# Moving the transposes' transfers off ScalarE's queue in a one-core encoder layer

## The chip, the cores and the metric

The kernel runs on one core of a Trainium2 chip. The metric is the device time of one execution in microseconds. Three runs of the kernel before took 1799.64, 1800.62 and 1801.30 us; the median is 1800.62 us.

## The reference

One encoder layer over 256 tokens of width 2048, all in float32:

```python
x = x + 0.5 * swiglu(rms_norm(x, ffn1_norm), ffn1_w_gu, ffn1_w_down)     # D_FF = 5632
proj = rms_norm(x, mix_norm) @ w_in                                      # 2048 x 4608
out_a = grouped-query attention, 8 query and 2 key heads of 128, q and k normed and rotated
out_b = differential attention, 4 heads: softmax map 0 minus lam * softmax map 1, o normed
x = x + concat(out_a, out_b) @ w_out
x = x + 0.5 * swiglu(rms_norm(x, ffn2_norm), ffn2_w_gu, ffn2_w_down)
x = rms_norm(x, out_norm)
```

Attention is bidirectional without a mask. All weights are read once, about 338 MB.

## The kernel before

**Matrix products.** Every float32 operand is split into a rounded part `hi` and a rest `lo`, and each product is three matmuls (lines 192 to 194): hi by hi, hi by lo, lo by hi. `mm_block` works on a block of the weights, 1024 columns wide. It goes through it in chunks of 256 rows: SyncE's queue (SP) loads a chunk (`raw`, line 173, three buffers), ScalarE (ACT) casts its two halves to `whi` (line 126, four buffers), VectorE (DVE) subtracts to get `wlo` (line 127), and TensorE (PE) runs 24 matmuls of 512 columns over it: two column halves, two token tiles, two row halves, three products.

**Interleaving.** Work that is not a matmul of the weights stands in a list, `pending`. `mm_block` takes entries from its front while it goes on: `slots` a chunk, 1 in the feed-forward parts and `MIX_SLOTS` in the mixer (`pump`). An empty entry (`lambda: None`) only spaces the list. The order of each engine's instructions is then set by a planner that simulates the engines and their queues, so an entry's place in the list is a priority rather than a fixed place. `issue_after(ins)` holds an instruction behind `ins` on its own engine. Each engine and each queue runs its instructions in the order that was written, and waits at the first one that is not ready.

**Transposes.** The activations `h` of the feed-forward part and the heads `q` and `k` of the mixer have to be turned. DVE transposes blocks of 32 by 32 (`turn`, lines 271 and 449), DMAs move the blocks between partitions (`move`, lines 277 and 453), and a copy or a split puts them in order (`order`, line 457; `parts`). ACT's queue begins all of these DMAs: 16 for each of the 12 groups of `h`, and 16 for each of the six head tiles (two token tiles of q of group A, k of group B and q of group B). The buffer `near` of the heads is single, so the second tile's transpose waits until the first tile's DMAs have read it.

**The mixer.** Its projection blocks run in the order k and v of A, q of A, k of B, q of B, v of B. After the last chunk of a block `qk_heads` norms and rotates the heads (ACT, DVE and GpSimd (POOL) in turn), and their turn is put into `pending`, to be done while the next block's matmuls run. The attention's stages (`scores`, `probs`, `values`, and `turn` for B) follow in the same list.

Of the kernel before, what the change touches and what calls it, by code (L numbers as in the profile page):

```python
# [28 lines left out]
B32 = 32  # L29
Q = P // B32  # L30
# [5 lines left out]
LAMBDA_INIT = 0.8 - 0.6 * math.exp(-0.3 * 0)  # L36
WB = 1024
WARM = 8
MIX_SLOTS = 3


@with_exitstack
def encoder_layer(ctx: ExitStack, tc: tile.TileContext, a: dict, out: bass.AP):
# [3 lines left out]
    nc = tc.nc  # L47
# [11 lines left out]
    def f32(ap):  # L59
        return ap.bitcast(F32)  # L60
# [22 lines left out]

    pending = collections.deque()

    def pump():
        if pending:
            pending.popleft()()

    def drain():  # L90
        while pending:
            pump()
# [30 lines left out]
                nc.gpsimd.tensor_tensor(self.rstd[t], ms, minus_half[:, :1], op=ALU.pow)  # L123

    def split(hi, lo, src):
        nc.scalar.copy(hi, src)  # L126
        return nc.vector.tensor_tensor(lo, src, f32(hi), op=ALU.subtract)  # L127

    def new_xT():
# [15 lines left out]
                nc.vector.scalar_tensor_tensor(lo[:, k + j, :], pj, gk, f32(hi[:, k + j, :]),  # L145
                                               op0=ALU.mult, op1=ALU.subtract)

    loads, splits = [], []

    def late_load(dst, src):  # L150

# [74 lines left out]
    def add_to_x(half, scale):  # L226
        def evac(b, t, ps, c0=0, c1=512):
            s = slice(half * WB + b * 512 + c0, half * WB + b * 512 + c1)
            nc.vector.scalar_tensor_tensor(x[t][:, s], ps[:, c0:c1], scale, x[t][:, s],  # L229
                                           op0=ALU.mult, op1=ALU.add)  # L230
        return evac


    def ffn(xT, norm, w_gu, w_down, half_done=None, before=None, after=None, last_evac=None, t_major=None):
        with tc.tile_pool(name="ffn", bufs=2) as fp:
            groups = [(c, min(WB, DFF - c)) for c in range(0, DFF, WB)]

            def gate(j):
                c, width = groups[j]
                sg = [fp.tile([P, WB], F32, name=f"sg{t}", bufs=1) for t in range(NT)]  # L240

                def evac(b, t, ps):
                    nc.scalar.activation(sg[t][:, b * 512:(b + 1) * 512], ps, AF.Silu,  # L243
                                         scale=norm.rstd[t][:, 0:1])
                if j == 0 and before is not None:
                    with tc.manual_schedule(engines={mybir.EngineType.SP}):
                        mm_block(xT, NK, w_gu, 0, c, width, evac, before, after)
                else:
                    mm_block(xT, NK, w_gu, 0, c, width, evac)
                return sg  # L250

            def up(j, sg):
                c, width = groups[j]
                h = [fp.tile([P, WB], F32, name=f"h{t}") for t in range(NT)]

                def evac(b, t, ps):
                    s = slice(b * 512, (b + 1) * 512)
                    nc.vector.scalar_tensor_tensor(h[t][:, s], ps, norm.rstd[t][:, 0:1], sg[t][:, s],  # L258
                                                   op0=ALU.mult, op1=ALU.mult)
                mm_block(xT, NK, w_gu, 0, DFF + c, width, evac)  # L260
                hT = (ht_p.tile([P, WB // P, T], F32R, name="hT_hi"),
                      ht_p.tile([P, WB // P, T], F32R, name="hT_lo"))
                nk = width // P
                n_ = nk * B32
                near = fp.tile([P, NT, Q, WB // Q], F32, name="near", bufs=1)[:, :, :, :n_]
                turned = fp.tile([P, NT, Q, WB // Q], F32, name="turned", bufs=1)[:, :, :, :n_]

                def turn(t):

                    with tc.issue_after(splits[-1].ins):  # L270
                        nc.vector.transpose(near[:, t].rearrange("p q (k d) -> p q k d", d=B32),  # L271
                                            h[t][:, :width].rearrange("p (k q d) -> p q k d", q=Q, d=B32))

                def move(i0):

                    for i, q in itertools.product(range(i0, i0 + 2), range(Q)):
                        nc.scalar.dma_start(turned[q * B32:(q + 1) * B32, :, i, :],
                                            near[i * B32:(i + 1) * B32, :, q, :])

                def parts(k):  # L280
                    src = turned.rearrange("p t i (k d) -> p (t i) k d", d=B32)[:, :, k:k + 2, :]
                    hi, lo = (part[:, k:k + 2, :].rearrange("p k (i d) -> p i k d", d=B32) for part in hT)
                    with tc.issue_after(splits[-1].ins):
                        split(hi, lo, src)

                pending.extend(functools.partial(turn, t) for t in range(NT))
                pending.append(lambda: None)
                pending.extend(functools.partial(move, i) for i in (0, 2))
                pending.append(lambda: None)
                pending.extend(functools.partial(parts, k) for k in range(0, nk, 2))  # L290
                pending.append(lambda: turned_groups.add(j))
                return hT

            def down(j, hT):
                c, width = groups[j]
                last = j == len(groups) - 1
                while j not in turned_groups:
                    pump()
                for half in range(2):
                    evac = last_evac(half) if last and last_evac else add_to_x(half, 0.5)  # L300
                    mm_block(hT, width // P, w_down, c, half * WB, WB, evac,
                             t_major=t_major if last and half == 1 else None)
                    if last and half_done:
                        half_done(half)

            n = len(groups)
            hT = {}
            turned_groups = set()
            for j in range(n):
                sg = gate(j)  # L310
                hT[j] = up(j, sg)
                if 0 < j < n - 1:
                    down(j - 1, hT.pop(j - 1))
            down(n - 2, hT.pop(n - 2))
            down(n - 1, hT.pop(n - 1))
# [39 lines left out]
    with ExitStack() as mixer:  # L355
# [86 lines left out]
        def turn_heads(o, dst):  # L442

            near = mw.tile([P, Q, 8, B32], F32, name="near", bufs=1)
            far = o.rearrange("p h d -> p (h d)").rearrange("p (i n) -> p i n", i=Q)

            def turn():
                with tc.issue_after(splits[-1].ins):
                    nc.vector.transpose(near, o.rearrange("p h (q d) -> p q h d", d=B32))

            def move():
                for i, q in itertools.product(range(Q), range(Q)):
                    nc.scalar.dma_start(far[q * B32:(q + 1) * B32, i],  # L453
                                      near[i * B32:(i + 1) * B32, q].rearrange("p h d -> p (h d)"))

            def order():
                nc.scalar.copy(dst.rearrange("p h (i d) -> p h i d", d=B32),
                               far.rearrange("p i (h d) -> p h i d", d=B32))
            pending.extend([turn, lambda: None, move, lambda: None, order])

        ka = []

# [141 lines left out]
        def new_oT():  # L604
            return (ht_p.tile([P, WB // P, T], F32R, name="hT_hi"),
                    ht_p.tile([P, WB // P, T], F32R, name="hT_lo"))

        w_in = a["w_in"]
        mm_block(xT2, NK, w_in, 0, 1024, 512, evac_kva, slots=MIX_SLOTS)
        mm_block(xT2, NK, w_in, 0, 0, WB, evac_qk("a", "q", qTa), slots=MIX_SLOTS)  # L610
        oTa = new_oT()
        s_, p_, v_ = zip(*[attn_a(h2, oTa) for h2 in range(4)])
        pending.extend([s_[0], s_[1], p_[0], s_[2], p_[1], v_[0], s_[3], p_[2], v_[1], p_[3], v_[2], v_[3]])
        mm_block(xT2, NK, w_in, 0, 2560, WB, evac_qk("b", "k", kTb), slots=MIX_SLOTS)
        qTb = mp.tile([P, 8, T], F32, name="qT")
        mm_block(xT2, NK, w_in, 0, 1536, WB, evac_qk("b", "q", qTb), slots=MIX_SLOTS)
        oTb = new_oT()
        s_, p_, v_, o_ = zip(*[attn_b(h, qTb, oTb) for h in range(4)])
        pending.extend([s_[0], s_[1], p_[0], s_[2], p_[1], s_[3], p_[2], p_[3]])
        mm_block(xT2, NK, w_in, 0, 3584, WB, evac_vb, slots=MIX_SLOTS)  # L620
        pending.extend([v_[0], v_[1], o_[0], v_[2], o_[1], v_[3], o_[2], o_[3]])
        for half in range(2):
            mm_block(oTa, 8, a["w_out"], 0, half * WB, WB, add_to_x(half, 1.0), slots=MIX_SLOTS)
        drain()
# [92 lines left out]
```

## Time and profile before

| | |
|---|---|
| median of three runs | 1800.62 us |
| the profiled execution | 1800.14 us |
| its span, first to last instruction | 1798.3 us |
| PE busy | 1775.8 us, 99% |
| DVE busy | 991.2 us, 55% |
| ACT busy | 829.2 us, 46% |
| POOL busy | 48.2 us, 3% |
| mean granted TensorE clock | 0.994 |

A busy share says how long an engine had an instruction at work. Matmuls are pipelined, so their durations overlap; their rate is read from how many start in a stretch. The granted clock is a share of full speed: 1.00 is 2.4 GHz. DMA-issuing instructions are not counted as busy time; in a timeline they stand under the engine's queue (ACTq, SPq). The mixer lies between about 735 and 1060 us of the span.

### The profile page before, as it was taken

To read this page: it belongs to the slowest core of one execution; us is meant where nothing else is said; L and a number is where in the kernel's file an instruction comes from. 1 tells how busy PE (TensorE), PEld (TensorE's weight loads), DVE (VectorE), ACT (ScalarE), POOL (GpSimd) and SP (SyncE) were. 2 spreads that over 40 slices of the span, in tenths; PEclk is the share of its full clock that TensorE was granted. 3 is DMA by queue.
4 is the path that set the end of the run, shared out by engine and by line. 5 is a ranking of instruction groups with operands and counts; after the bars stand their busy time and mean duration, and the time that the engine had idled before them with its cause. 6 is when DMAs were issued, how large, how long until landed. Compare 5 with 4: busy or idle time off the path is not lost.

```text
span 1798.3 us, 20478 instructions
## 1 busy us (share of the span) xinstructions
PE 1775.8 (99%) x7864; PEld 1466.0 (82%) x7864; DVE 991.2 (55%) x1147; ACT 829.2 (46%) x1195; POOL 48.2 (3%) x75
## 2 busy tenths in 40 slices
PE   9999999999999999999989999999999999999998
PEld 7888888888888888887778888888888888888886
DVE  6454645645545657754455664545645645545556
ACT  6443443443443444655766454343443443444444
POOL 0000000000000000130120000000000000000000
PEclk9999999999999999998999999999999999999999
DMA  9565655655656575655444455666656656656573
GB/s 343 195 210 190 223 196 188 213 198 196 212 193 206 164 242 188 211 168 184 162 156 173 165 186 187 197 216 205 202 191 210 207 188 214 204 190 211 153 253 121
DMA packets 117635, 355.73 MB, mean 198 GB/s; under 512 B 10992, under 2 KB 27808, under 8 KB 117408
## 3 DMA queue, kind: packets, MB, share of 16 engines
q1 hardware_dynamic: 96752, 338.39, 56.6%
q10 hardware_dynamic: 20688, 16.01, 3.2%
q8 instruction: 61, 1.00, 0.2%
q14 instruction: 38, 0.31, 0.1%
q0 software_dynamic: 96, 0.02, 0.0%
HBM read 337.60 MB, written 2.10 MB: 189 GB/s over the span
## 4 chain that ended last, share of the span: by engine, by line
PE 94%; ACT 2%; DMA 1%; DVE 1%; issue 1%; ACTq 0%; POOL 0%; DVEq 0%; POOLq 0%
PE psm L193 31%; PE psm L194 31%; PE psm L192 31%; DMA raw<-in_w_in 1%; ACT heads L422 0%; DVE wlo L127 0%; ACT whi L126 0%; DMA raw<-in_w_out 0%; PE psx L139 0%; PE psx L580 0%; ACT heads L440 0%; ACTq L453 0%; PE psx L525 0%; PE psx L560 0%; PE psx L545 0%
## 5 line engine op out<-in xcount | busy, mean ns | idle before, releaser
L127 DVE TENSOR_TENSOR wlo<-raw,whi 128x1024 fp32r<-128x1024 f32 (+1 forms) x676 | 756.7, 1153 | 683.7 <-ACT whi L126 680.0
L126 ACT CAST whi<-raw 128x1024 fp32r<-128x1024 f32 (+1 forms) x676 | 646.9, 996 | 818.8 <-PE psm L194 725.1
L193 PE MATMUL psm<-wlo,xT_hi 128*128 128x512 f32 x1696 | 662.4, 392 | 2.6 <-DVE wlo L127 2.5
L194 PE MATMUL psm<-whi,xT_lo 128*128 128x512 f32 x1696 | 659.0, 391 | 0.0
L192 PE MATMUL psm<-whi,xT_hi 128*128 128x512 f32 x1696 | 586.6, 392 | 9.1 <-ACT whi L126 7.7
L192 PEld LDWEIGHTS psm<-whi,xT_hi 128*128 128x128 f32 x1696 | 319.5, 189 | 77.8 <-ACT whi L126 9.2
L193 PEld LDWEIGHTS psm<-wlo,xT_hi 128*128 128x128 f32 x1696 | 319.7, 189 | 71.5 <-DVE wlo L127 5.2
L194 PEld LDWEIGHTS psm<-whi,xT_lo 128*128 128x128 f32 x1696 | 319.6, 188 | 66.0
L193 PE MATMUL psm<-wlo,hT_hi 128*128 128x512 f32 x836 | 323.4, 389 | 0.0
L194 PE MATMUL psm<-whi,hT_lo 128*128 128x512 f32 x836 | 323.4, 389 | 0.0
L192 PE MATMUL psm<-whi,hT_hi 128*128 128x512 f32 x836 | 293.8, 388 | 0.0
L193 PEld LDWEIGHTS psm<-wlo,hT_hi 128*128 128x128 f32 x836 | 157.0, 188 | 32.3
L192 PEld LDWEIGHTS psm<-whi,hT_hi 128*128 128x128 f32 x836 | 157.0, 188 | 32.1
L194 PEld LDWEIGHTS psm<-whi,hT_lo 128*128 128x128 f32 x836 | 157.0, 188 | 31.9
L229 DVE SCALAR_TENSOR_TENSOR x<-psm,x 128x512 f32<-128x512 f32 (+1 forms) x113 | 73.9, 680 | 16.0 <-PE psm L194 15.0
L123 POOL TENSOR_TENSOR rstd<-ms,minus_half 128x1 f32<-128x1 f32 x8 | 4.6, 575 | 1487.1 <-DVE ms L122 1487.1
L126 ACT CAST hT_hi<-turned 128x512 fp32r<-128x512 f32 x44 | 24.1, 617 | 39.2 <-DMA turned<-near 39.2
L243 ACT ACTIVATE sg<-psm,rstd 128x512 f32<-128x512 f32 x44 | 28.6, 687 | 12.5 <-PE psm L194 12.5
L258 DVE SCALAR_TENSOR_TENSOR h<-psm,rstd,sg 128x512 f32<-128x512 f32 x44 | 31.6, 737 | 0.0
L127 DVE TENSOR_TENSOR hT_lo<-turned,hT_hi 128x512 fp32r<-128x512 f32 x44 | 30.1, 684 | 0.0
L501 ACT ACTIVATE e<-psx,nb 128x256 f32<-128x256 f32 x32 | 14.8, 472 | 29.4 <-DMA heads<-near 24.7
L271 DVE STREAM_TRANSPOSE near<-h 128x1024 f32<-128x1024 f32 (+1 forms) x24 | 27.6, 1151 | 0.3
(101 smaller groups left out, 386.4 us busy)
## 6 DMA issues: line engine op xcount, KB each, us to landing
raw<-in_ffn_w_gu SPq DMA_DIRECT2D x158, 1024.0 KB, 5.0
raw<-in_ffn_w_down SPq DMA_DIRECT2D x88, 1024.0 KB, 5.0
raw<-in_w_in SPq DMA_DIRECT2D x32, 1024.0 KB, 5.2
raw<-in_ffn_w_gu SPq DMA_DIRECT2D x32, 512.0 KB, 3.7
raw<-in_w_out SPq DMA_DIRECT2D x16, 1024.0 KB, 4.9
turned<-near ACTq DMA_DIRECT2D x160, 64.0 KB, 4.2
raw<-in_w_in SPq DMA_DIRECT2D x8, 512.0 KB, 3.7
heads<-near ACTq DMA_DIRECT2D x96, 32.0 KB, 3.1
```

Source lines behind the costliest of these rows:

```text
L123: nc.gpsimd.tensor_tensor(self.rstd[t], ms, minus_half[:, :1], op=ALU.pow)
L126: nc.scalar.copy(hi, src)
L127: return nc.vector.tensor_tensor(lo, src, f32(hi), op=ALU.subtract)
L192: nc.tensor.matmul(o, xh, wh, start=k == 0, stop=False)
L193: nc.tensor.matmul(o, xh, wl, start=False, stop=False)
L194: nc.tensor.matmul(o, xl, wh, start=False, stop=k == nk - 1)
L229: nc.vector.scalar_tensor_tensor(x[t][:, s], ps[:, c0:c1], scale, x[t][:, s], op0=ALU.mult, op1=ALU.add)
L243: nc.scalar.activation(sg[t][:, b * 512:(b + 1) * 512], ps, AF.Silu, scale=norm.rstd[t][:, 0:1])
L258: nc.vector.scalar_tensor_tensor(h[t][:, s], ps, norm.rstd[t][:, 0:1], sg[t][:, s], op0=ALU.mult, op1=ALU.mult)
L271: nc.vector.transpose(near[:, t].rearrange("p q (k d) -> p q k d", d=B32), h[t][:, :width].rearrange("p (k q d) -> p q k d", q=Q, d=B32))
L501: nc.scalar.activation(e[:, m, :], sv[:, m, :], AF.Exp, bias=nb[:, m:m + 1], scale=SCALE, accum_out=sm[:, m:m + 1])
```

## The change

`h`'s DMAs are begun by POOL's queue, and the heads' DMAs by SP's, which carries the weight loads too. The heads' 16 DMAs become four entries of four instead of one entry, with three empty entries behind them, and the final copy is held behind ACT's latest cast. `MIX_SLOTS` goes from 3 to 4, and the attention's lists get empty entries. The number and the size of the transfers, and all arithmetic, stay as they are.

```diff
-MIX_SLOTS = 3
+MIX_SLOTS = 4
...
+    def idle():
+        pass
...
     def split(hi, lo, src):
-        nc.scalar.copy(hi, src)
+        casts.append(nc.scalar.copy(hi, src))
...
                     for i, q in itertools.product(range(i0, i0 + 2), range(Q)):
-                        nc.scalar.dma_start(turned[q * B32:(q + 1) * B32, :, i, :],
+                        nc.gpsimd.dma_start(turned[q * B32:(q + 1) * B32, :, i, :],
                                             near[i * B32:(i + 1) * B32, :, q, :])
...
-            def move():
-                for i, q in itertools.product(range(Q), range(Q)):
-                    nc.scalar.dma_start(far[q * B32:(q + 1) * B32, i],
+            def move(i):
+                for q in range(Q):
+                    nc.sync.dma_start(far[q * B32:(q + 1) * B32, i],
                                       near[i * B32:(i + 1) * B32, q].rearrange("p h d -> p (h d)"))
 
             def order():
-                nc.scalar.copy(dst.rearrange("p h (i d) -> p h i d", d=B32),
-                               far.rearrange("p i (h d) -> p h i d", d=B32))
-            pending.extend([turn, lambda: None, move, lambda: None, order])
+                with tc.issue_after(casts[-1].ins):
+                    nc.scalar.copy(dst.rearrange("p h (i d) -> p h i d", d=B32),
+                                   far.rearrange("p i (h d) -> p h i d", d=B32))
+            pending.extend([turn, idle] + [functools.partial(move, i) for i in range(Q)] + [idle] * 3 + [order])
...
-        pending.extend([s_[0], s_[1], p_[0], s_[2], p_[1], v_[0], s_[3], p_[2], v_[1], p_[3], v_[2], v_[3]])
+        pending.extend([s_[0], idle, idle, s_[1], p_[0], idle, v_[0], s_[2], p_[1], idle, v_[1], s_[3], p_[2], idle,
+                        v_[2], idle, p_[3], idle, v_[3]])
...
-        pending.extend([s_[0], s_[1], p_[0], s_[2], p_[1], s_[3], p_[2], p_[3]])
+        pending.extend([s_[0], idle, idle, s_[1], p_[0], idle, s_[2], p_[1], idle, s_[3], p_[2], idle, idle, p_[3]])
```

## Rows read from the trace of the kernel before

**Rows 1.** The page, busy time of each engine, its share and its instructions.
```profile
PE 1775.8 (99%) x7864; PEld 1466.0 (82%) x7864; DVE 991.2 (55%) x1147; ACT 829.2 (46%) x1195; POOL 48.2 (3%) x75
```
**Rows 2.** Stretches: length, busy time (count) by engine, PE clock, DMA share, GB/s.
```profile
100.00:200.00 100.00, 100.00 (x443) 82.81 (x442) 50.89 (x48) 41.07 (x45) 0.00 (x0) 1.00 0.65 215
...
820.00:840.00 20.00, 17.30 (x58) 13.39 (x59) 8.53 (x10) 8.57 (x12) 0.00 (x0) 0.74 0.42 136
```
**Rows 3.** Waits of PE: who waited for whom, total us, times, longest.
```profile
PE psm L192 <- ACT whi L126: 7.7, 4, 3.7
PE psm L193 <- DVE wlo L127: 2.5, 3, 1.6
...
PE psx L509 <- ACT e L501: 1.2, 1, 1.2
```
**Rows 4.** Timeline of PE: start, us, instruction, count, [idle before it <- releaser].
```profile
810.35 1.07 PE L192 MATMUL psm<-whi,xT_hi 128*128 128x512 f32 x4
...
818.29 0.39 PE L194 MATMUL psm<-whi,xT_lo 128*128 128x512 f32 x1
821.95 2.08 PE L192 MATMUL psm<-whi,xT_hi 128*128 128x512 f32 x4 [3.28 <-ACT whi L126]
...
935.74 1.28 PE L192 MATMUL psm<-whi,xT_hi 128*128 128x512 f32 x4 [3.71 <-ACT whi L126]
```
**Rows 5.** Stretches as in Rows 2, the two stalls of PE.
```profile
818.50:830.90 12.40, 8.37 (x19) 6.01 (x19) 5.76 (x5) 4.83 (x5) 0.00 (x0) 0.59 0.48 156
...
931.80:943.70 11.90, 6.63 (x18) 4.72 (x17) 5.76 (x5) 4.83 (x5) 0.00 (x0) 0.71 0.33 99
```
**Rows 6.** Timeline of ACT and its queue around the stalls.
```profile
809.49 1.04 ACT L126 CAST whi<-raw 128x1024 fp32r<-128x1024 f32 x1
809.59 3.12 ACTq L453 DMA_DIRECT2D heads<-near  x5
...
814.49 6.33 ACTq L453 DMA_DIRECT2D heads<-near  x9
820.86 2.94 ACT L126 CAST whi<-raw 128x1024 fp32r<-128x1024 f32 x3 [6.39 <-DMA heads<-near]
...
884.27 0.47 ACT L501 ACTIVATE e<-psx,nb 128x256 f32<-128x256 f32 x1 [3.12 <-DMA heads<-near]
...
934.65 2.94 ACT L126 CAST whi<-raw 128x1024 fp32r<-128x1024 f32 x3 [6.77 <-DMA heads<-near]
```
**Rows 7.** Timeline of DVE, the second head tile's transpose.
```profile
822.37 1.25 DVE L449 STREAM_TRANSPOSE near<-heads 128x1024 f32<-128x1024 f32 x1 [9.30 <-DMA heads<-near]
```
**Rows 8.** Line 453, the heads' DMAs: ns of an issue, us to landing (min/median/max).
```profile
L453 ACTq DMA_DIRECT2D heads<-near x96: 513/602/716, 809.6 to 949.8; - x96
...
DMA to landing us min/median/max: 1.8/3.1/6.6
```
**Rows 9.** The chain that ended last, a weight load in the first stall.
```profile
810.69 5.74 DMA raw<-in_w_in
```
**Rows 10.** Waits of SP's queue, columns as in Rows 3.
```profile
SPq L173 <- DVE wlo L127: 1363.3, 296, 9.8
```
**Rows 11.** Line 173, the weight loads on SP, columns as in Rows 8.
```profile
L173 SPq DMA_DIRECT2D raw<-in_w_in x40: 367/368/379, 707.6 to 939.7; - x40
```
**Rows 12.** Timeline of ACT and its queue in the feed-forward part, one group's turn.
```profile
98.37 1.45 ACTq L277 DMA_DIRECT2D turned<-near  x2
...
115.42 2.19 ACT L126 CAST hT_hi<-turned 128x512 fp32r<-128x512 f32 x4 [4.18 <-DMA turned<-near]
...
120.12 2.01 ACT L126 CAST whi<-raw 128x1024 fp32r<-128x1024 f32 x2 [0.61 <-PE psm L194]
```
**Rows 13.** Line 70, DMAs begun by POOL, columns as in Rows 8.
```profile
L70 POOL DMA_DIRECT2D gain_ffn_norm<-in_ffn_norm x2: 534/635/736, 1.3 to 2.6; - x2
...
DMA to landing us min/median/max: 4.4/5.2/5.4
```
**Rows 14.** Groups by line and shape: count, busy us, mean ns, idle before.
```profile
L127 DVE TENSOR_TENSOR wlo<-raw,whi 128x1024 fp32r<-128x1024 f32 x588 | 696.7, 1222 | 635.5 <-ACT whi L126 634.7
```

More of the change, by code (lines that the diff above doesn't have):

```diff
@@ L146, in fill_xT @@
                                                op0=ALU.mult, op1=ALU.subtract)
-    loads, splits = [], []
+    loads, splits, casts = [], [], []
     def late_load(dst, src):
@@ L286, in up @@
                 pending.extend(functools.partial(turn, t) for t in range(NT))
-                pending.append(lambda: None)
+                pending.append(idle)
                 pending.extend(functools.partial(move, i) for i in (0, 2))
-                pending.append(lambda: None)
+                pending.append(idle)
                 pending.extend(functools.partial(parts, k) for k in range(0, nk, 2))
```

## The prediction

> **What bounds the kernel now.** I read the busy shares first. PE has an instruction at work for 1775.8 us of a span of 1798.3 [rows 1], so only time in which PE stands still or runs slowly can be won. The stretches come next: in the feed-forward part PE starts 443 matmuls in 100 us at a granted clock of 1.00, one in 0.2257 us, and never idles; between 820 and 840 us the clock is 0.74 [rows 2]. PE's waits name the places: 7.7 us for `whi`, 2.5 us for `wlo`, 1.2 us for the softmax's `e`, 11.4 us in all [rows 3]. PE's timeline shows two of them at length, 3.28 us before the matmuls at 821.95 and 3.71 us before those at 935.74 [rows 4]. The reader is to see there that four matmuls after the first take 2.08 us, where four took 1.07 us at 810.35: after the stop PE runs at the lower of its two levels, 1.2 instead of 2.4 GHz, for a while.
>
> A stop therefore costs more than its idle time, and I price both by the count. From 818.50 to 830.90 there are 19 matmuls in 12.40 us; at full rate they take 19 x 0.2257 = 4.29, so 8.1 us are lost. From 931.80 to 943.70 it is 18 in 11.90 us, 4.06 at full rate, 7.8 us lost [rows 5]. PE is idle for 12.40 - 8.37 = 4.03 and 11.90 - 6.63 = 5.27 us of these two; the other 8.11 - 4.03 = 4.1 us of the first is the clock's. Of the 11.4 us of waits, 11.4 - 9.3 = 2.1 us lie elsewhere. The most that the change can win is 8.1 + 7.8 + 2.1 = 18.0 us.
>
> Why is `whi` late? ACT casts half a chunk at 809.49 and the next at 820.86. Between them its queue issues DMAs of the head turn: 5 in 3.12 us, later 9 in 6.33 us, and the wait before the cast is put down to the transfers [rows 6]. One issue takes 0.602 us [rows 8], so 16 take 9.6 us of ACT's order, ahead of a cast that could have run soon after PE left the old chunk at 810.35 [rows 4]. The second stall has the same picture (6.77 us before the casts at 934.65), and `e` at 884.27 sat 3.12 us behind the third block's issues [rows 6]. ACT is not overloaded; its casts stand behind issues in one queue.
>
> **The change part by part.**
>
> Heads' DMAs to SP. ACT loses 16 x 0.602 = 9.6 us of issue in each of six turns. The cast of 820.86 can then start some 10 us earlier, near 811, and PE needs it at 818.5 [rows 4, 6]. I count the whole 18.0 us as removable; all three places have the same cause.
>
> What is late next is a wait that stays. The second tile's transpose stood 9.30 us on DVE until the first tile's transfers had landed [rows 7], and SP won't issue these faster: from 809.59, 16 x 0.602 and about 3.1 to land [rows 8] give 822.3, the same instant. Before, no `wlo` could pass it because no cast had run. Now `wlo` must stand ahead of that transpose in DVE's order, and the same goes for the casts and the final copy on ACT. The planner orders by when things are ready in its own simulation; a transpose that is ready late goes late, so I take nothing for this and keep the case as a rival.
>
> SP is the queue moved past. It spends most of its time waiting for DVE to free a load's buffer, 1363.3 us [rows 10], and a load's issue takes only 0.367 us [rows 11], so it has room on average. Within a turn it has not: 16 moves fill 9.6 us, in which a load can come due. The tight one is the load issued at 810.69, 5.74 us to landing [rows 9]. Behind all moves of the first tile it goes at 809.59 + 9.6 = 819.2 and lands at 825.0; a cast of 1.04 us [rows 6] ends at 826.0 and `wlo` of 1.22 us [rows 14] at 827.2. PE wants that chunk three chunks of 24 x 0.2257 = 5.42 us after 810.35, at 826.6, and its `wlo` four matmuls later, at 827.5. It comes 0.6 and 0.3 us early. So the cost lies between nothing and, if it is later, its lateness and 4.1 us of slow clock. The row it is nearest to is nothing; I charge 0.5 us in each of the three blocks, 1.5 us.
>
> `h`'s DMAs to POOL. They free ACT of 16 issues in each of 12 groups, but PE never idles there [rows 2], so the gain is nothing. What covers the cost of the slower path is the planned distance: the first issue was at 98.37 and the casts that read the result ran at 115.42 [rows 12]. POOL's only DMAs took 0.534 to 0.736 us each and 5.2 to land [rows 13]; 16 of the slowest end at 98.37 + 11.8 + 5.2 = 115.4, no later than now. The bound above: the turned casts (2.19 us) and a weight cast must be through by 120.12, when PE takes the next chunk, so the read may slip to 116.9, which is 0.83 us an issue. Nothing else uses POOL there.
>
> A rule of the Trainium skill speaks against this part, and the row for it is DVE's rate: `wlo` takes 1222 ns for 1024 elements a partition, 1.19 ns each [rows 14]. SBUF — State Buffer, "SBUF: two separate sides", says that a DMA from POOL's queue cannot get its descriptors written while DVE holds the port that the two share, in a two-port mode. The same page, "Who interferes with whom", says that a tensor_tensor has no such mode. By the first alone the sum would gain the time of the last rival below; by the second nothing. No row shows a POOL DMA beside a busy DVE.
>
> Wider spacing, four slots, the copy behind the latest cast. They add no instruction on PE, DVE or ACT. A feed of 20 turn entries and 19 stage entries against 32 a block leaves seven for the next block, which then needs 7 + 20 = 27 of 32: it still fits. PE's one wait for `e`, 1.2 us [rows 3], is in the 2.1 already counted. Nothing is taken for them.
>
> **The sum.** 1800.14 (profiled execution) - 18.0 + 1.5 = 1783.6, which I call 1784. The median of the runs stands 0.5 us above the profiled execution, which would make it 1784.1.
>
> **The rivals.**
>
> One stop stays: in one of the two long places something in order (DVE's transpose, ACT's copy) still stands before what PE needs, and in the other not. 1783.6 + 8 = about 1792. For it: the second transpose is ready at the same 822.3 as before. Against it: casts are ready ten microseconds before that.
>
> The wait only moves: both long stops stay, behind the transpose or the copy, and only the 2.1 us go. 1800.14 - 2.1 = 1798.0. For it, the 9.30 us on DVE; against it, that the planner put the copy behind four casts before.
>
> Slower, SP's order: a weight load stands behind the moves of the second tile, which wait for its transpose. That ends at 822.37 + 1.25 = 823.6; 16 issues and a landing of 5.74 later it is 839.0, and cast at 840.0, where PE wanted 826.6: 13.4 + 4.1 = 17.5 us a block. In two of three blocks: 1800.14 - 16.5 + 35 = 1819. It decides once a load stands more than 0.3 us later than worked out above. For it: moves precede those loads in the list. Against it: the load is ready first, its buffer being freed at 810.69.
>
> Slower, POOL: an issue takes over 0.83 us. At 1.0 us the read comes at 119.6, 2.7 us late, with the clock 6.8 us, in ten groups 68 us: about 1850. If each issue waited for one DVE instruction, 0.64 + 1.22 = 1.86 us, it would be 16.4 + 4.1 = 20.5 us a group, near 1990. For it: 16 strided DMAs were never begun there. Against it: the three rows of POOL.
>
> **How the numbers follow.** Forecast 0.56 (its own range 1781 to 1789), one stop stays 0.13, the wait moves 0.14, SP 0.12, POOL 0.05. Three runs differ by 1.7 us, so about 0.2%, 3.6 us, is what can be told from no change. Faster than 1797: the first two and a third of the third (0.05), 0.74. Within: the rest of it and a single lost block of SP, 0.10. Slower: 0.16. From 1780 to 1800 lie the first three cases, 0.83.
>
> **What would show it.** Right: no wait of PE above 1 us between 800 and 960, clock 1.00 throughout that stretch, casts about 5.4 us a pair apart, no DMA issue on ACT's queue between 735 and 1060. The feed-forward stretches stay at 443 matmuls in 100 us. Wrong: a wait of PE for `wlo` with DVE idle before line 449; a wait for `whi` with ACT before line 457, or with a load landing late; in the feed-forward part, idle time of PE, with ACT before the turned casts.

## The result and the profile after

| | before | after |
|---|---|---|
| median, us | 1800.96 | 1782.91 |
| lowest to highest, us | 1799.64 to 1801.48 | 1782.46 to 1784.27 |
| the profiled execution, us | 1800.14 | 1782.46 |
| its span, us | 1798.3 | 1780.7 |
| mean granted TensorE clock | 0.994 | 0.999 |

The ratio is 0.9902, with an interval of 0.9885 to 0.9919: 1% faster. The forecast was 1784, with 1781 to 1789 for the likeliest case alone. Every ratio here compares fast runs; one of the ten executions with only `h`'s DMAs on POOL took 6404.25 us at full clock, for a cause that no profile shows, and is in that kernel's median but not in its ratio.

The page after, busy times; the columns are those of [rows 1]:

```profile
PE 1767.7 (99%) x7864; PEld 1462.4 (82%) x7864; DVE 990.4 (56%) x1147; ACT 829.2 (47%) x1195; POOL 149.5 (8%) x267
```

PE has the same 7864 matmuls and 8.1 us less busy time; most of it, (8.37 - 4.29) + (6.63 - 4.06) = 6.65 us, is what ran at the lower clock level in the two stalls of [rows 5]. DVE's and ACT's busy time is the same within 1 us. POOL has 192 DMAs more, 101 us that PE never waits for.

The stretches after, as in [rows 2]; 920 to 940 holds what answers to the second stop of [rows 5]:

```profile
100.00:200.00 100.00, 100.00 (x443) 82.80 (x442) 52.08 (x49) 41.12 (x45) 15.63 (x30) 1.00 0.66 216
820.00:840.00 20.00, 20.00 (x90) 16.58 (x89) 9.12 (x10) 11.28 (x20) 0.60 (x2) 1.00 0.64 222
840.00:860.00 20.00, 18.43 (x85) 14.66 (x84) 12.34 (x24) 18.54 (x64) 7.07 (x9) 1.00 0.55 204
920.00:940.00 20.00, 20.00 (x92) 16.66 (x91) 12.57 (x15) 10.23 (x15) 0.00 (x0) 1.00 0.45 147
```

The feed-forward part does the same 443 matmuls in 100 us. Both long stops are gone, and with them the clock of 0.74. All of PE's waits after (those of [rows 3] and two at the start of the kernel):

```profile
PE psm L195 <- ACT whi L129: 1.5, 1, 1.5
PE psm L195 <- ACT xT_hi L330: 1.5, 1, 1.5
PE psx L80 <- DVE parts L116: 1.2, 1, 1.2
```

None of the waits that made up the 11.4 us is left. The 1.5 us for `whi`, at 854, are new: PE of the kernel before has no wait between 825 and 885. The next two timelines show the place of the first stop. On ACT, the answer to [rows 6]:

```profile
809.54 2.14 ACT L129 CAST whi<-raw 128x1024 fp32r<-128x1024 f32 x2
...
816.06 1.06 ACT L129 CAST whi<-raw 128x1024 fp32r<-128x1024 f32 x1 [0.59 <-PE psm L197]
821.30 1.05 ACT L461 COPY qT<-heads 128x1024 f32<-128x1024 f32 x1 [4.18 <-DMA heads<-near]
825.22 1.99 ACT L129 CAST whi<-raw 128x1024 fp32r<-128x1024 f32 x2 [2.86 <-DMA raw<-in_w_in]
```

The two casts at 809.54 run back to back; the second of them stood at 820.86 before. The final copy waits for the transfers, but behind the casts that PE needs. On SP:

```profile
807.09 0.37 SPq L176 DMA_DIRECT2D raw<-in_w_in  x1
809.65 10.10 SPq L456 DMA_DIRECT2D heads<-near  x16
819.85 1.56 SPq L176 DMA_DIRECT2D raw<-in_w_in  x3
822.68 13.52 SPq L456 DMA_DIRECT2D heads<-near  x16
836.30 20.84 SPq L176 DMA_DIRECT2D raw<-in_w_in  x5
```

All 16 moves of a tile stand in one row, and three loads wait behind them. The second tile's 16 take 13.52 us, 3.4 more than the first's: in the trace the seventh and the eighth of them go only when a load ahead has landed, at 827.67 and 830.57. The next loads stand behind these moves and go at 836.30. DVE, the answer to [rows 7]:

```profile
817.15 1.23 DVE L130 TENSOR_TENSOR wlo<-raw,whi 128x1024 fp32r<-128x1024 f32 x1 [0.42 <-ACT whi L129]
821.41 1.25 DVE L452 STREAM_TRANSPOSE near<-heads 128x1024 f32<-128x1024 f32 x1 [3.03 <-DMA heads<-near]
```

The second transpose runs 1 us earlier than before and still waits for the transfers, now behind the `wlo` of the chunks that had stopped PE.

### The profile page after: what moved, and what is told of

It is laid out like the page before. It is cut to its first block, busy times and chain, and to the rows that moved or that the text cites. A ratio compares the mean times of both kernels' runs of the same rounds, so it can differ in the third digit from the quotient of the medians.

```text
span 1780.7 us, 20561 instructions
## 1 busy us (share of the span) xinstructions
PE 1767.7 (99%) x7864; PEld 1462.4 (82%) x7864; DVE 990.4 (56%) x1147; ACT 829.2 (47%) x1195; POOL 149.5 (8%) x267
## 4 chain that ended last, share of the span: by engine, by line
PE 95%; ACT 1%; DMA 1%; SPq 1%; DVE 1%; issue 1%; POOL 0%; POOLq 0%; ACTq 0%; DVEq 0%
PE psm L196 31%; PE psm L197 31%; PE psm L195 31%; DMA raw<-in_w_in 1%; SPq L456 1%; PE psx L142 0%; PE psx L549 0%; PE psx L564 0%; PE psx L584 0%; ACT heads L425 0%; ACT heads L443 0%; PE psx L513 0%; DMA gain_ffn_norm<-in_ffn_norm 0%; ACT q_sb L422 0%; ACT whi L129 0%
## 5 line engine op out<-in xcount | busy, mean ns | idle before, releaser
L280 POOL DMA_DIRECT2D turned<-near x192 | 101.3, 535 | 1204.6 <-DVE near L274 1020.0
L104 POOL TENSOR_TENSOR rs<-ms,minus_half 128x4 f32<-128x4 f32 (+1 forms) x18 | 20.2, 1120 | 116.6 <-DVE ms L103 116.5
L120 ACT ACTIVATE junk<-x 128x512 bf16<-128x512 f32 (+1 forms) x33 | 20.3, 614 | 16.4 <-DVE x L232 14.2
```

The costliest lines, as they stand in the source:

```text
L104: nc.gpsimd.tensor_tensor(dst, ms[:, :width], minus_half[:, :width], op=ALU.pow)
L120: nc.scalar.activation(junk[:, :c1 - c0], x[t][:, c0:c1], AF.Square, scale=D ** -0.5, accum_out=p[:, n:n + 1])
L280: nc.gpsimd.dma_start(turned[q * B32:(q + 1) * B32, :, i, :], near[i * B32:(i + 1) * B32, :, q, :])
```

## The experiments

Two theories stood against each other at first. Q: what counts is that the heads' DMAs are issued by ACT's queue, ahead of the weight casts. S: what counts is the wider spacing of the list.

**The heads' queue alone.**

```diff
# the kernel before
-                    nc.scalar.dma_start(far[q * B32:(q + 1) * B32, i],
+                    nc.sync.dma_start(far[q * B32:(q + 1) * B32, i],
```

> The kernel before with one edit: the heads' 96 DMAs are begun by SP's queue. One entry of 16 moves, three slots, the old lists, h's DMAs still on ACT. Theory Q (the 16 x 0.602 us of issue stood ahead of the weight casts on ACT, and the queue is what matters): both long stops of PE go, about 1783 to 1788 us. Theory S (the wider spacing of the list is what matters): the stops stay, 1797 to 1803 us.

Measured: 1782.71 us, ratio 0.9902 (0.9887 to 0.9917). One word gives the whole change. Its SP timeline is that of the changed kernel:

```profile
809.51 10.09 SPq L453 DMA_DIRECT2D heads<-near  x16
819.70 1.55 SPq L173 DMA_DIRECT2D raw<-in_w_in  x3
```

Cutting the moves into four list entries with an empty one here and there has not spread them: the planner takes them as soon as they are ready.

**The spacing alone.**

```diff
# the changed kernel
-                        nc.gpsimd.dma_start(turned[q * B32:(q + 1) * B32, :, i, :],
+                        nc.scalar.dma_start(turned[q * B32:(q + 1) * B32, :, i, :],
...
-                    nc.sync.dma_start(far[q * B32:(q + 1) * B32, i],
+                    nc.scalar.dma_start(far[q * B32:(q + 1) * B32, i],
```

> The changed kernel with all of its DMAs back on ACT's queue: four slots, moves in four entries, empty entries and the held copy stay. Theory Q: the issues still stand ahead of the casts, PE stops remain, 1793 to 1803 us. Theory S: about 1783 us.

Measured: 1800.17 us, ratio 0.9994 (0.9985 to 1.0004). ACT shows the picture of [rows 6] again:

```profile
816.04 6.27 ACTq L456 DMA_DIRECT2D heads<-near  x9
822.35 2.94 ACT L129 CAST whi<-raw 128x1024 fp32r<-128x1024 f32 x3 [6.33 <-DMA heads<-near]
```

and PE waits for `whi` as before:

```profile
PE psm L195 <- ACT whi L129: 6.8, 4, 3.2
```

S falls, by both runs: without the spacing the whole gain is there, and with the spacing alone none of it.

**`h`'s queue, alone and taken back.**

```diff
# the kernel before (first), and the reverse in the changed kernel (second)
-                        nc.scalar.dma_start(turned[q * B32:(q + 1) * B32, :, i, :],
+                        nc.gpsimd.dma_start(turned[q * B32:(q + 1) * B32, :, i, :],
```

> The kernel before with h's 192 DMAs begun by POOL's queue and nothing else. Theories Q and S: PE has no idle time in the feed-forward parts to win, and the read comes no later than before, so 1799 to 1802 us. Rival P (POOL's issue takes over 0.83 us): slower, 1810 to 1850 us.

> The changed kernel with h's DMAs back on ACT's queue; the heads on SP and the spacing stay. Theory Q: as the changed kernel, 1782 to 1785 us, since the mixer has no h DMA. A theory in which the freed ACT of the feed-forward part pays: 1788 us or more.

Measured: 1802.02 us, ratio 1.0004 (0.9994 to 1.0014), and 1783.47 us, ratio 0.9904 (0.9889 to 0.9918). POOL's part of the change neither wins nor costs anything that can be told.

**One block back.**

```diff
# the changed kernel
-        def turn_heads(o, dst):
+        def turn_heads(o, dst, eng):
...
-                    nc.sync.dma_start(far[q * B32:(q + 1) * B32, i],
+                    eng.dma_start(far[q * B32:(q + 1) * B32, i],
...
+                turn_heads(heads[t], dst[:, :, t * P:(t + 1) * P],
+                               nc.scalar if grp + n == "bq" else nc.sync)
```

> The changed kernel with the DMAs of one of the three blocks, q of group B, back on ACT's queue. Theory Q: that block's stop of PE (7.8 us lost before, at 932 us) and the short one behind it come back alone, 1789 to 1793 us, with the lower clock level after it and none in the block of q of group A. Rival (the stops hang together through the list): under 1785 or over 1797 us.

Measured: 1793.16 us, ratio 0.9957 (0.994 to 0.9973), 10.3 us over the changed kernel and 0.16 us past the end of the range. The stretches of this kernel, as above:

```profile
820.00:840.00 20.00, 20.00 (x90) 16.57 (x89) 9.30 (x11) 9.37 (x14) 0.00 (x0) 1.00 0.58 195
920.00:940.00 20.00, 15.38 (x56) 11.54 (x55) 6.45 (x6) 6.87 (x10) 0.00 (x0) 0.83 0.50 165
```

The stop comes back in its own block and nowhere else, with the lower clock after it.

**Half of the issues back.**

```diff
# the changed kernel
-                    nc.sync.dma_start(far[q * B32:(q + 1) * B32, i],
+                    (nc.sync if q % 2 == 0 else nc.scalar).dma_start(far[q * B32:(q + 1) * B32, i],
```

> The changed kernel with half of the heads' DMAs, 8 of 16 a tile, back on ACT's queue and 8 on SP's. Theory Q with a threshold: 8 x 0.602 = 4.8 us ahead of the cast that could run at about 811 and is wanted by 818.5 still fit, and SP's loads wait half as long, so 1781 to 1786 us. Rival D (the loss is in proportion to the issues on ACT): half of the 18 us come back, 1789 to 1794 us.

Measured: 1791.18 us, ratio 0.995 (0.9935 to 0.9964). The number is the rival's, the mechanism is not. ACT's cast is early enough, as the threshold has it; then DVE's order gives it away. ACT, DVE and PE of this kernel:

```profile
818.23 2.94 ACT L129 CAST whi<-raw 128x1024 fp32r<-128x1024 f32 x3 [1.96 <-DMA heads<-near]
```
```profile
823.24 1.25 DVE L452 STREAM_TRANSPOSE near<-heads 128x1024 f32<-128x1024 f32 x1 [8.36 <-DMA heads<-near]
824.41 3.45 DVE L130 TENSOR_TENSOR wlo<-raw,whi 128x1024 fp32r<-128x1024 f32 x3
```
```profile
820.33 1.07 PE L195 MATMUL psm<-whi,xT_hi 128*128 128x512 f32 x4
825.65 0.66 PE L196 MATMUL psm<-wlo,xT_hi 128*128 128x512 f32 x1 [4.25 <-DVE wlo L130]
```

The transpose that waits for the transfers was put ahead of the `wlo` whose cast ends at 819.2. This is the prediction's case "one stop stays", seen at work: with that cast some 6 us earlier (the changed kernel, whose trace runs 1.7 us ahead of this one) the same transpose stands behind them and costs nothing. That the later cast is what made the planner put the transpose first is argued, not shown. The other two blocks have eight issues a tile on ACT as well, and no wait of PE there reaches 1 us.

**SP's issues doubled.**

```diff
# the changed kernel
-                for q in range(Q):
-                    nc.sync.dma_start(far[q * B32:(q + 1) * B32, i],
-                                      near[i * B32:(i + 1) * B32, q].rearrange("p h d -> p (h d)"))
+                for q, c in itertools.product(range(Q), (slice(0, 128), slice(128, 256))):
+                    nc.sync.dma_start(far[q * B32:(q + 1) * B32, i, c],
+                                      near[i * B32:(i + 1) * B32, q].rearrange("p h d -> p (h d)")[:, c])
```

> The changed kernel with each of the heads' DMAs cut into two of half the size: 32 issues on SP a tile instead of 16. The trace of the changed kernel has the load of chunk 6 at 819.85, right behind 16 moves (809.65, 10.10 us), its cast at 825.22, and PE wanting it at about 826.6. Theory E (that load stands at the edge, and the moves stay ahead of it): about 10 us more of issue put it some 9 us too late, 9 + 4 = 13 us a block in two or three blocks, 1805 to 1825 us. Rival R (the planner lets the loads pass the moves once these take longer, or the loads have more room than I worked out): 1782 to 1788 us.

Measured: 1822.83 us, ratio 1.012 (1.0105 to 1.0135): slower than the kernel before, within theory E's range. The matmuls that take chunk 6, in the changed kernel:

```profile
827.63 1.09 PE L195 MATMUL psm<-whi,xT_hi 128*128 128x512 f32 x4
```

ACT, SP and PE of this kernel, same place:

```profile
831.23 1.04 ACT L461 COPY qT<-heads 128x1024 f32<-128x1024 f32 x1 [14.26 <-DMA heads<-near]
835.40 1.99 ACT L129 CAST whi<-raw 128x1024 fp32r<-128x1024 f32 x2 [3.13 <-DMA raw<-in_w_in]
```
```profile
809.52 20.22 SPq L456 DMA_DIRECT2D heads<-near  x32
829.84 1.55 SPq L176 DMA_DIRECT2D raw<-in_w_in  x3
```
```profile
832.33 2.08 PE L529 MATMUL psx<-kTa,qT 128*128 128x256 f32 x4 [5.57 <-ACT qT L461]
836.50 2.07 PE L195 MATMUL psm<-whi,xT_hi 128*128 128x512 f32 x4 [2.10 <-ACT whi L129]
```

The load is 10 us later, as expected; its cast moves by 10.2 us (825.22 to 835.40) and the matmuls that need it by 8.9 (827.63 to 836.50), so in this place the load had 1.3 us of room. But PE stops first for the scores, which stand ahead of the late matmuls in its own order and wait for the copied heads (5.57 us), and only then for the cast (2.10 us). So the lateness is right, and its first victim was not the one I named. The waits of PE in the whole kernel:

```profile
PE psx L529 <- ACT qT L461: 9.4, 2, 5.6
PE psx L564 <- ACT qT L461: 7.5, 2, 4.4
PE psm L195 <- ACT whi L129: 5.1, 3, 2.5
```

16.9 us are waits for the copied heads, whose own 32 transfers take 20 us to issue, and 5.1 us waits for `whi`. Here PE meets the heads first and the late cast after them, so the cast alone would have stopped it too. Theory E named only the loads; how much of the 40 us over the changed kernel is theirs is not shown.

**POOL's issues doubled.**

```diff
# the changed kernel
-                    for i, q in itertools.product(range(i0, i0 + 2), range(Q)):
-                        nc.gpsimd.dma_start(turned[q * B32:(q + 1) * B32, :, i, :],
-                                            near[i * B32:(i + 1) * B32, :, q, :])
+                    for i, q, t in itertools.product(range(i0, i0 + 2), range(Q), range(NT)):
+                        nc.gpsimd.dma_start(turned[q * B32:(q + 1) * B32, t, i, :],
+                                            near[i * B32:(i + 1) * B32, t, q, :])
```

> The changed kernel with each of h's DMAs cut into two, one a token tile: 32 issues on POOL a group instead of 16. Theory E (the read of the turned rows stays where it is in ACT's order, at 116.64, with 0.3 us to spare): 32 x 0.533 = 17.1 us of issue instead of 8.5 and two more waits of 2.5 us for earlier transfers put it some 9 us late, with the clock 13 us in ten groups, about 1900 us. Rival R (the planner's order gives way, since the groups' results are wanted much later): 1782 to 1788 us.

Measured: 1783.14 us, ratio 0.9898 (0.9884 to 0.9913). Theory E falls. The read of the turned rows in the changed kernel; below it POOL's last issues and the read in this one:

```profile
116.64 2.18 ACT L129 CAST hT_hi<-turned 128x512 fp32r<-128x512 f32 x4
```
```profile
114.97 0.98 POOL L280 DMA_DIRECT2D turned<-near  x2 [2.19 <-DMA turned<-near]
```
```profile
128.94 2.18 ACT L129 CAST hT_hi<-turned 128x512 fp32r<-128x512 f32 x4
```

The last issues move to 115 and the read to 128.94, some two chunks of PE further on: the planner gave the longer chain its time.

**The heads on POOL.**

```diff
# the changed kernel
-                    nc.sync.dma_start(far[q * B32:(q + 1) * B32, i],
+                    nc.gpsimd.dma_start(far[q * B32:(q + 1) * B32, i],
```

> The changed kernel with the heads' DMAs on POOL's queue instead of SP's. SP then has only loads and the load of chunk 6 goes at about 811 again. Theory Q (off ACT's queue is all that counts): 1781 to 1785 us. Rival N (POOL's swaps and powers of the norms stand behind moves that wait for a transpose, so the head chain and with it the casts come late): one to three stops of about 8 us, 1790 to 1805 us.

Measured: 1792.58 us, ratio 0.9954 (0.9939 to 0.9969), in the rival's range, 9.7 us over SP, so being off ACT's queue is not all that counts. The stops are neither the old ones (820 to 840 runs at full rate) nor the rival's of about 8 us: PE has eight waits between 905 and 1013, 7.9 us together, the longest 3.28 us. POOL's moves wait for earlier ones to land and mix with the norms' powers, so the second tile's moves begin at 833.17 instead of 822.68, and the attention of group B comes later too:

```profile
833.17 3.91 POOL L456 DMA_DIRECT2D heads<-near  x8 [10.14 <-DVE near L452]
```
```profile
1004.24 0.48 PE L513 MATMUL psx<-ident,e 128*128 128x128 f32 x1 [3.28 <-DVE e L573]
```

The late turn and the stop near 1004 are seen; that the one causes the other is argued, not shown.

**No moves at all.**

```diff
# the changed kernel
-            pending.extend([turn, idle] + [functools.partial(move, i) for i in range(Q)] + [idle] * 3 + [order])
+            pending.extend([turn, idle] + [idle] * 7 + [order])
```

> The changed kernel without the heads' DMAs at all: the blocks of q and k are transposed but not moved between partitions, so the attention works on heads in the wrong places. Theory Q: the changed kernel has already won all that the transfers cost, 1781 to 1783.5 us, with the one stop of about 1.5 us at 854 us still there. Rival (the moves on SP still cost PE time by late loads or copies): under 1780 us.

Measured: 1781.01 us (1780.25 to 1782.54), ratio 0.9894 (0.9878 to 0.9911). The time is as expected; the stop at 854 is gone, which I had expected to stay. So that stop is a price of the moves. All that they still cost is 1782.91 - 1781.01 = 1.9 us, which is little more than can be told: this kernel's slowest run (1782.54) is slower than the changed kernel's fastest (1782.46).

## Why the prediction was right

**The removable loss.** I counted 8.1 + 7.8 + 2.1 = 18.0 us. Without the moves the kernel is 1800.55 - 1781.01 = 19.5 us faster than the kernel before, measured beside it. The interval of that ratio runs from 16 to 22 us, so the 1.5 us more are not clear of noise. Some of them are an error of the count: a stretch counts matmuls that were still running when it began. From start to start, 19 matmuls go from 818.29 to 830.91 and 17 from 931.64 to 943.73, which makes 8.3 us lost in each stall, 16.6 instead of 15.9. Where the rest comes from was not found.

**Heads' DMAs to SP.** The cast came "near 811": 810.6. The load, worked out to go at 819.2 and land at 825.0, went at 819.85, and its cast began at 825.22. PE did not stop for it, as the 0.6 us of room said; the doubled issues put the room at 1.3 us. They turn 18 us of gain into 22 us of loss, but the heads are late there as well as the loads, so the size of that loss says nothing of the edge.

**The charge of 1.5 us** stands against the 1.9 us just measured, but in one place, not three: PE waits 1.51 us at 854, with ACT before a cast in the middle of the head norms:

```profile
841.97 2.00 ACT L129 CAST whi<-raw 128x1024 fp32r<-128x1024 f32 x2 [1.47 <-DMA raw<-in_w_in]
853.11 1.99 ACT L129 CAST whi<-raw 128x1024 fp32r<-128x1024 f32 x2
854.21 1.20 PE L195 MATMUL psm<-whi,xT_hi 128*128 128x512 f32 x4 [1.51 <-ACT whi L129]
```

ACT works without a gap from 841.97 to that cast, and the stretch begins with a cast that waited for the load sent at 836.30, behind the second tile's moves. That is the order of the rival "SP's order", on later loads than the one it priced; that this lateness is what delays the cast at 853.11 is argued from the order, and shown only so far that the stop goes when the moves go. The gain was 1.5 us too small and the cost 0.4 us too small, so a part of the error cancels, by luck: 17.7 us between the profiled executions, 16.5 forecast.

**The wait that stays.** The second transpose still waits for the transfers, 3.03 instead of 9.30 us, and the planner put it late, as I took it to. It starts at 821.41, 0.9 us before the 822.3 worked out: on SP the heads' DMAs land 1.9 us after they are begun (median), not 3.1. The run with half of the issues shows what it costs where it does not.

**`h`'s DMAs to POOL.** Gain and cost are nothing, as forecast, and one issue takes 0.533 us, the lower end of [rows 13]:

```profile
L280 POOL DMA_DIRECT2D turned<-near x192: 533/533/612, 98.7 to 1723.7; - x192
```

The bound of 0.83 us an issue was wrong as a bound. It took the read's place in ACT's order as fixed; doubled, the issues took more than that, and the read moved by 12.3 us at no cost. The last rival's price would therefore hold only where the planner does not know of the delay; no run shows that. Beside DVE at 52% in these stretches POOL's longest issue was 0.612 us. That hangs together with what the Trainium skill, SBUF — State Buffer, "Who interferes with whom", says of tensor_tensor, that it has no two-port mode. The trap that the same page of the Trainium skill tells of in "SBUF: two separate sides" was not tried here: in the changed kernel's trace the only DVE instructions that run beside these issues are the tensor_tensor of line 130.

**The spacing.** Taken at nothing, and it is: 1782.71 without it, 1782.91 with it.

**The signs.** Of the signs named for being right, the clock is 1.00 from 800 to 960, ACT's queue issues no DMA between 735 and 1060, and the feed-forward stretch keeps its 443 matmuls. Two did not come: PE has one wait above 1 us, at 854, and the casts are not 5.4 us a pair apart, as the gap from 816.06 to 825.22 shows.

## What to carry to other kernels

Count every DMA that is issued from a compute engine's queue at its full issue time, in that engine's order, and look at what stands behind it: here 16 issues of 0.6 us held one cast by 10 us on an engine that was 46% busy. When they are moved to another queue, do the same sum there, since the loads behind them had only about 1 us of room (0.6 by the sum, 1.3 by the doubled run). And where a planner sets the order, test a margin by doubling the suspected work before calling it a bound, and read from the trace which wait grew.

## What the runs showed that I had not expected

- POOL's issues were no dearer than SP's: 0.533 us for 64 KB on POOL, 0.588 us for 32 KB on SP and 0.602 us on ACT, all at 32 partitions. With the heads on POOL its 32 KB took 0.496 us. The weight loads of 1024 KB took 0.368 us on SP, so the bytes alone do not set it.
- With 16 or 32 DMAs in a row POOL stops for earlier ones to land, 2.46 us after 14 of them in the changed kernel. In the trace the fifteenth waits for a semaphore that the landing of the seventh sets, at 108.33, so the wait is in the program's order of semaphores; whether the queue itself would have to stop is not shown.
- Half the issues on ACT cost as much as one whole block's: 1791.18 against 1793.16 us. The loss is not in proportion to the number of issues: most of it comes from the one place where the transpose stands ahead of the `wlo`.
